# First mixer of a two-layer trunk: convolution input in a PSUM bank, one pair of convolution blocks inside the first pass, roots by eight heads, later transposes

## Chip, cores and metric

The kernel runs on one core of one Trainium2 chip. The metric is the device time of one execution in microseconds. Inputs and weights lie in device memory, in layouts that the kernel's packing on the host has chosen; that packing is not timed.

## What is computed

A trunk of two layers over 256 tokens of width 2048. Each layer is a mixer and a feed-forward network, each with an RMS norm whose scale, shift and gate come from a conditioning vector (`mod = silu(c) @ ada_w + ada_b`). The change lies in the first layer's mixer:

```python
def even_mixer(h, ...):
    z = h @ w_in
    a, q, kc, vc, ks, vs, kw, vw, gl = split_cols(z, EVEN_SPLITS)   # 2048, 1024, 6 x 256, 24
    y_a = conformer_conv(a, conv_w, conv_b, conv_ln_g, conv_ln_b)
    y_b = nsa_attention(q, kc, vc, ks, vs, kw, vw, gl, ...)
    return concatenate([y_a, y_b], axis=-1) @ w_out

def conformer_conv(a, w_dw, b_dw, ln_g, ln_b):
    a1, a2 = split(a, 2, axis=-1)                                   # value and gate, 1024 channels each
    y = causal_dwconv(a1 * sigmoid(a2), w_dw, b_dw)                 # 31 taps per channel, along the tokens
    return silu(layer_norm(y, ln_g, ln_b))
```

`nsa_attention` norms and rotates 8 heads of q and the keys k_sel and k_win (2 heads of 128 each), compresses k_cmp and v_cmp by a small network over windows of 32 tokens, and adds three gated attentions per head. All is float32.

## The kernel before

Tokens are one tile of 256 (NT = 2 halves of 128); channels go in blocks of 128 partitions, and the width of 2048 is 16 k-tiles. Activations `h(kt)` are kept transposed. `mm_t` (L350) makes a transposed output block, 128 channels by 256 tokens; `mm_n` (L361) makes outputs with tokens on the partitions.

**Weights.** `Weights` holds a list of loads in the order of use. `load_to` (L116) issues each from SyncE's queue into one of three `raw` buffers; `take` hands over the next piece and keeps the loads ahead. Conditioning weights come through the same queue: `ada()` (L263) reduces one 128x2048 tile on VectorE (L269), 192 times in all, and then issues the next load into the buffer just read (L260), so such a load waits on the queue for VectorE, with all that stands behind it.

**What sets the order.** Each engine runs its instructions in the order in which the program issues them. The helper `take` (L319) issues side work at each weight piece: deferred steps (`advance`), the next entry of the lists `hooks` and `beside` (`hook`), and by rate constants some `jobs` and some `ada()` (`tick`, L300). A rate of 0.5 is one per two takes. The constants at L55 to L80 are such rates, by stage.

**The first mixer, in order.**
1. The first pass (L776 to L787): one loop over the 16 k-tiles accumulates in eight PSUM banks: `oc` (two blocks of k_cmp, a bank each), `ok` (k_sel and k_win) and `oq` (q).
2. Four fills of convolution blocks. `fill` (L888) projects one block; the first of a pair is the gate (`sg`, tanh on ScalarE, L894), the second the value, after which `taps` (L899) writes `xp` = (sg + 1) * value (L904).
3. The values of the attention: `proj_n` with 268 columns, twice; beside it the keys and queries are finished: `squares` (ScalarE, L592), `roots` (L1021, one reciprocal root over all 24 heads on VectorE), `scaled` (L596), `roped` (two products on GpSimd, then L605 and L606 on VectorE), `turned_in` (transposes on PE, L613). All these stand in `hooks`, one per take; the three `turned_in` are entries 9, 11 and 13.
4. Two blocks of v_cmp, the compression of k_cmp (`hidden`, L849; `hs`, L861), two fills, that of v_cmp.
5. Ten fills, and beside them the heads: `stage_a` and `stage_b`, one per take. They hold the scores, the exponentials (L1173) and the transposes, whose results are copied by VectorE (`pT`, L1198) and ScalarE (L1199, L1200), then PE's outputs (L1209).
6. The output projection, whose first blocks need attention only; then the sums for the layer norm of the convolution (`cs`, L979; PE's L986), and the rest.

**A convolution block** takes 31 taps of 128x256, each reading a shifted window of `xp`, cut into six jobs: 10 taps by ScalarE (`pr`, L919), which GpSimd adds up (`yp`, L921), and 21 by VectorE into two accumulators in turn (`cy`, `ye`; L926, L928, L930). `xp` lies in SBUF in two buffers, so `taps` forces only the jobs of the block before last:

```python
            while c > 1 and c - 2 not in tapped:
                jobs.pop(0)()
            xp = xps[c % 2]
```

Of the kernel before, what the change touches and what calls it, by code (L numbers as in the profile page):

```python
# [54 lines left out]
LO_A = 0.25  # L55
ADA_A = 0.25
CONV_A = 0
CONV_1 = 0.7
CONV_2 = 2.0
CONV_3 = 1.2  # L60
CONV_OUT = 4
PRE = 5
SP = (7, 10)
# [2 lines left out]
LO_2 = 0.25  # L66
LO_3 = 0.25
LO_T = 0.25
ADA_T = 0.4
LO_F = 0.25  # L70
ADA_1 = 0.5
ADA_2 = 0.5
ADA_3 = 0.6
ADA_F0S = 0.45
ADA_F0U = 0.42
ADA_F0D = 0.22
ADA_L1 = 0.0
# [75 lines left out]
def trunk(ctx, tc, a, out):  # L153
# [6 lines left out]
    wp = ctx.enter_context(tc.tile_pool(name="wp", bufs=3))  # L160
    hm = ctx.enter_context(tc.tile_pool(name="hm", bufs=12))
    sm = ctx.enter_context(tc.tile_pool(name="sm", bufs=2))
    psum = ctx.enter_context(tc.tile_pool(name="psum", bufs=8, space=bass.MemoryType.PSUM))

    def bank():
        return psum.tile([P, 512], F32, tag="bank", name="bank")


    cc = const.tile([P, 3, P], F32, name="cc")
# [35 lines left out]
                W.want(a["wdn"][i, q, kt], QK, P)  # L205

    for kt in range(KD):
        W.want(a["ev_1"][kt], 1, 1792, cuts=(768, 1024), split=False)
    def want_pairs(c0, c1):
        for c in range(c0, c1):  # L210
            for ab in (1, 0):
                W.want(a["ev_a"][2 * c + ab], KD, P, split=False)
# [2 lines left out]
        for u in range(4):  # L215
            W.want_raw(a["cmp_w1"][kv, :, u * 2048:(u + 1) * 2048], 2048)

    want_pairs(0, 2)
    for c in range(2):
        W.want(a["ev_v"][c], KD, 268, split=False)  # L220
    for g in range(2):
# [121 lines left out]
    def mm_t(o, w, s_, x, start, stop):  # L343
        if isinstance(w, tuple):
            hi, lo = w
            PE.matmul(o, hi[:, s_], x[:, 0], start=start, stop=False)  # L346
            PE.matmul(o, hi[:, s_], x[:, 1], start=False, stop=False)  # L347
            PE.matmul(o, lo[:, s_], x[:, 0], start=False, stop=stop)  # L348
        else:
            PE.matmul(o, w[:, s_], x, start=start, stop=stop)  # L350

    def mm_n(o, w, s_, x, start, stop):
        for t in range(NT):
            ts_ = slice(t * P, (t + 1) * P)
            if isinstance(w, tuple):
                hi, lo = w
                PE.matmul(o[t], x[:, 0, ts_], hi[:, s_], start=start, stop=False)
                PE.matmul(o[t], x[:, 0, ts_], lo[:, s_], start=False, stop=False)
                PE.matmul(o[t], x[:, 1, ts_], hi[:, s_], start=False, stop=stop)
            else:  # L360
                PE.matmul(o[t], x[:, ts_], w[:, s_], start=start, stop=stop)  # L361
# [232 lines left out]
    def head_scale(z, nh, r, gain, n):  # L594
        for h in range(nh):
            V.scalar_tensor_tensor(n[:, h], z[:, h], r[:, h:h + 1], gain(h), op0=ALU.mult, op1=ALU.mult)  # L596
# [134 lines left out]
    nc.sync.dma_start(posi, a["pos"])  # L731
    nc.sync.dma_start(inv, a["inv"].partition_broadcast(P))
    V.memset(onesm, 1.0)
    make_identity(nc, ident)

    for u in range(4):
# [33 lines left out]
    table = tables()  # L770
    h = Modulated(0, 0, whole=True)
    h.bc = on_all(token_rstd())
    oc = [bank()[:, :T] for _ in range(2)]
    ok = [bank() for _ in range(NT)]
    oq = [[bank() for _ in range(NT)] for _ in range(2)]
    for kt in range(KD):  # L776
        x = h(kt)
        if kt > 1:
            next(table, None)
        first, stop = kt == 0, kt == KD - 1  # L780
        w, _ = take()
        for g in range(2):
            mm_t(oc[g], w, slice(g * P, (g + 1) * P), x, first, stop)
        mm_n(ok, w, slice(256, 768), x, first, stop)
        w, _ = take()
        for c in range(2):
            mm_n(oq[c], w, slice(c * 512, (c + 1) * 512), x, first, stop)  # L787
# [9 lines left out]
    with tc.tile_pool(name="l0", bufs=2) as lp:  # L797
# [81 lines left out]

        ys = []  # L880
        glu = []
        xps = [lp.tile([P, 30 + T], F32, name=f"xp{u}", bufs=1) for u in range(2)]
        for xp in xps:
            G.memset(xp[:, :30], 0.0)
        norm = {}
        count, totals, tapped = [0], [], set()

        def fill():  # L888

            o = proj_t(h)  # L890
            if count[0] % 2 == 0:
                sg = lp.tile([P, T], F32, tag="sg", name="sg")
                glu.append(sg)
                defer(lambda: S.activation(sg, o, AF.Tanh, scale=0.5))  # L894
            else:
                defer(lambda: taps(o))
            count[0] += 1

        def taps(o):  # L899
            c = len(ys)  # L900
            while c > 1 and c - 2 not in tapped:
                jobs.pop(0)()
            xp = xps[c % 2]
            V.scalar_tensor_tensor(xp[:, 30:], glu.pop(0), 1.0, o, op0=ALU.add, op1=ALU.mult)  # L904

            y = lp.tile([P, T], F32, tag="cy", name="cy", bufs=8)
# [101 lines left out]
        def activated(c):  # L1008
            S.activation(mix(c), ys[c], AF.Silu, bias=cvw[:, c, 33:34], scale=cvw[:, c, 32:33])
# [7 lines left out]
        def squares(i):  # L1017
            for u in (2 * i, 2 * i + 1):
                head_squares(zs[u], 4, s24[:, u])

        def roots():  # L1021
            flat = s24.rearrange("p a b -> p (a b)")
            V.tensor_scalar(flat, flat, 1.0 / P, EPS, op0=ALU.mult, op1=ALU.add)
            r = rsqrt(flat, 24)
            V.tensor_scalar(r[:, 8:], r[:, 8:], SCALE, None, op0=ALU.mult)
            root.append(r)

        def scaled(i):
            n = hm.tile([P, NT, 4, P], F32, tag="hm", name="n")
            ns.append(n)  # L1030
            gain = (lambda j: gains[:, 0]) if i else (lambda j: gains[:, 2 + j // 2])
            for t in range(NT):
                u = 2 * i + t
                head_scale(zs[u], 4, root[0][:, 4 * u:4 * u + 4], gain, n[:, t])

        later = []

        def roped_rest():
            while later:
                later.pop(0)()  # L1040
# [13 lines left out]
                    S.activation(qT[i - 1][:, :, t * P:(t + 1) * P], p, AF.Copy)  # L1054

        hooks.append(lambda: (squares(0), adds[0]()))
        hooks.append(lambda: (squares(1), adds[1]()))
        hooks.append(lambda: (squares(2), masks()))
        hooks.append(roots)
        hooks.append(lambda: scaled(0))  # L1060
        hooks.append(lambda: (scaled(1), roped(0)))
        hooks.append(lambda: (scaled(2), roped_rest()))
        hooks.append(lambda: roped(1))
        hooks.append(lambda: (turned_in(0), roped_rest()))
        hooks.append(lambda: roped(2))
        hooks.append(lambda: (turned_in(1), roped_rest()))
        hooks.append(None)
        hooks.append(lambda: turned_in(2))
        rate.update(ada=ADA_A, jobs=CONV_A)
        W.share = LO_A  # L1070
        for _ in range(4):
            fill()
        rate.update(ada=ADA_1, jobs=CONV_1)
        W.share = LO_1
# [175 lines left out]
        def ready(c):  # L1250
# [3 lines left out]
            if c < 7:  # L1254
# [2 lines left out]
        drain()  # L1257
        rest = out_first(0, mix, 1, [finish, None, layer_stats, layer_scale, lambda: normed(0),
                                      lambda: (normed(1), activated(0))], ready, ADA_OUT)

    h = ffn(0, rest, None, ADA_F0S, ADA_F0U, ADA_F0D)

# [228 lines left out]
def layout(inputs):  # L1491
# [48 lines left out]
    w = x["ev_w_in"][0]  # L1540
    s = dict(zip("a q kc vc ks vs kw vw gl".split(), np.split(w, np.cumsum([2048, 1024] + [256] * 6), axis=1)))
    a["ev_a"] = blocks(s["a"]).reshape(2, 8, P, D).transpose(1, 0, 2, 3).reshape(16, P, D)
    a["ev_1"] = np.concatenate([s["kc"], s["ks"], s["kw"], s["q"]], axis=1).reshape(KD, P, 1792)
    v = np.concatenate([s["vs"], s["gl"], s["vw"]], axis=1)
    a["ev_v"] = np.stack([rows(v[:, :268]), rows(v[:, 268:])])
    a["ev_c"] = blocks(s["vc"])
# [42 lines left out]
```

## Time and profile before

| what | before |
|---|---|
| runs, median (lowest to highest of 3) | 2412.89 us (2411.61 to 2413.17) |
| the profiled execution | 2410.45 us, its span 2408.7 us |
| PE busy | 2303.3 us, 96% |
| VectorE, ScalarE, GpSimd busy | 1663.0, 1029.5, 575.0 us |
| moved by DMA | 597.66 MB |
| first mixer, first pass to the sums of the convolution | 30.8 to 430 us of the span |

Times of the trace count from the start of the span. In a timeline row stand the start, the length, the engine, the line, the operation with its tiles, and xN where N like instructions are one row; a float32 matmul is two records, so a block of 16 products is 32 records. In square brackets stands how long the engine had been idle and what released it.

### The profile page before, as it was taken

What the parts mean: (1) busy time and instruction counts of PE and PEld (TensorE: products, weight loads), DVE (VectorE), ACT (ScalarE), POOL (GpSimd) and SP (SyncE); (2) the same over time, 40 slices, a digit from 0 to 9 for tenths busy, and PEclk for the clock granted to TensorE, in tenths of its full rate; (3) what the DMA queues carried; (4) which work ended last, traced back from release to release, by engine and by line L of the source; (5) the groups of instructions that cost most, each with busy time, mean ns of one, the idle gap of its engine ahead of it and who ended that gap; (6) DMA issues with size and microseconds to landing.
All of it is one profiled execution on the core that took longest, in us unless ns stands there. A gap on an engine that the chain in (4) does not pass through costs nothing. (4 is left out here: it accounts for less than half of the span.)

```text
span 2408.7 us, 39982 instructions
## 1 busy us (share of the span) xinstructions
PE 2303.3 (96%) x16052; PEld 2134.6 (89%) x16052; DVE 1663.0 (69%) x2587; ACT 1029.5 (43%) x1803; POOL 575.0 (24%) x329
## 2 busy tenths in 40 slices
PE   6899999898999999999999999999999999999999
PEld 3476778788999999999999877999999999999999
DVE  7758689738968877877887467555786554554554
ACT  2021253125434544544544545446534444444443
POOL 4233534001322222222222131110222212222221
PEclk9999999999999999999999999999999999999999
DMA  9968754866879878878888542444577545545545
GB/s 387 427 224 334 300 187 166 307 226 261 334 273 355 329 275 334 341 274 315 345 309 295 194 158 105 156 168 179 214 269 271 191 156 201 186 157 204 182 165 169
DMA packets 96525, 597.66 MB, mean 248 GB/s; under 512 B 11345, under 2 KB 14033, under 8 KB 44241
## 3 DMA queue, kind: packets, MB, share of 16 engines
q1 hardware_dynamic: 96338, 595.10, 66.8%
q8 instruction: 126, 2.06, 0.3%
q14 instruction: 61, 0.50, 0.1%
HBM read 592.96 MB, written 2.10 MB: 247 GB/s over the span
## 5 line engine op out<-in xcount | busy, mean ns | idle before, releaser
L133 ACT ACTIVATE whi<-raw 128x1024 fp32r<-128x1024 f32 (+2 forms) x659 | 626.4, 952 | 859.1 <-PE bank L347 727.9
L139 DVE TENSOR_TENSOR wlo<-raw,whi 128x1024 fp32r<-128x1024 f32 (+2 forms) x495 | 560.1, 1133 | 410.5 <-ACT whi L133 410.2
L139 POOL TENSOR_TENSOR wlo<-raw,whi 128x1024 fp32r<-128x1024 f32 (+2 forms) x164 | 389.4, 2374 | 1558.8 <-ACT whi L133 1504.5
L348 PE MATMUL bank<-h,wlo 128*128 128x256 f32 x2624 | 745.7, 284 | 9.5 <-DVE wlo L139 8.7
L346 PE MATMUL bank<-h,whi 128*128 128x256 f32 x2624 | 745.4, 284 | 0.0
L347 PE MATMUL bank<-h,whi 128*128 128x256 f32 x2624 | 744.7, 284 | 0.0
L348 PEld LDWEIGHTS bank<-h,wlo 128*128 128x128 f32 x2624 | 506.0, 193 | 10.8 <-DVE wlo L139 9.8
L346 PEld LDWEIGHTS bank<-h,whi 128*128 128x128 f32 x2624 | 506.3, 193 | 0.1
L347 PEld LDWEIGHTS bank<-h,whi 128*128 128x128 f32 x2624 | 506.2, 193 | 0.1
L269 DVE CUSTOM_DVE_ANT_0 ada<-ada,cB,adab 128x2048 f32<-128x2048 f32 x192 | 462.5, 2412 | 28.9 <-DMA ada<-adaw 28.2
L347 PE MATMUL bank<-g,whi 128*128 128x256 f32 x1408 | 403.4, 286 | 8.7 <-DVE g L662 8.5
L346 PE MATMUL bank<-g,whi 128*128 128x256 f32 x1408 | 402.9, 286 | 6.7 <-ACT g L661 5.9
L348 PE MATMUL bank<-g,wlo 128*128 128x256 f32 x1408 | 403.5, 287 | 4.4 <-DVE wlo L139 3.1
L347 PEld LDWEIGHTS bank<-g,whi 128*128 128x128 f32 x1408 | 274.3, 195 | 10.3 <-DVE g L662 10.3
L346 PEld LDWEIGHTS bank<-g,whi 128*128 128x128 f32 x1408 | 274.2, 195 | 7.7 <-ACT g L661 6.7
L348 PEld LDWEIGHTS bank<-g,wlo 128*128 128x128 f32 x1408 | 274.4, 195 | 6.4 <-DVE wlo L139 3.8
L350 PE MATMUL bank<-hw,raw 128*128 128x256 f32 x640 | 149.0, 387 | 10.7 <-DMA raw<-ev 7.9
L350 PEld LDWEIGHTS bank<-hw,raw 128*128 128x128 f32 x640 | 121.5, 194 | 38.9 <-issue 18.3
L350 PE MATMUL bank<-hr,raw 128*128 128x257 f32 x640 | 140.4, 380 | 0.0
L650 DVE SCALAR_TENSOR_TENSOR y<-bank,fcw,y 128x255 f32<-128x255 f32 x162 | 77.4, 478 | 90.2 <-ACT y L649 90.2
L350 PEld LDWEIGHTS bank<-hr,raw 128*128 128x128 f32 x640 | 121.0, 190 | 16.6
L350 PE MATMUL bank<-mixw,raw 128*128 128x256 f32 x512 | 115.7, 389 | 6.5 <-DMA raw<-out 6.5
(261 smaller groups left out, 2492.5 us busy)
## 6 DMA issues: line engine op xcount, KB each, us to landing
ada<-adaw SPq DMA_DIRECT2D x192, 1024.0 KB, 5.8
raw<-wup SPq DMA_DIRECT2D x162, 1024.0 KB, 6.3
raw<-wdn SPq DMA_DIRECT2D x128, 704.0 KB, 4.8
raw<-out SPq DMA_DIRECT2D x44, 512.0 KB, 4.2
raw<-ev_a SPq DMA_DIRECT2D x16, 1024.0 KB, 5.6
raw<-ev SPq DMA_DIRECT2D x16, 896.0 KB, 14.7
raw<-wup SPq DMA_DIRECT2D x16, 896.0 KB, 4.5
raw<-cmp_w SPq DMA_DIRECT2D x8, 1024.0 KB, 9.2
```

Source lines behind the costliest of these rows:

```text
L133: nc.scalar.activation(hi[:, :n], raw, AF.Copy)
L139: eng.tensor_sub(lo[:, :n], raw, hi[:, :n].bitcast(F32))
L269: V.tensor_tensor_reduce(w, w, cB, 1.0, adab[:, i * 96 + j:i * 96 + j + 1], ALU.mult, ALU.add, m)
L346: PE.matmul(o, hi[:, s_], x[:, 0], start=start, stop=False)
L347: PE.matmul(o, hi[:, s_], x[:, 1], start=False, stop=False)
L348: PE.matmul(o, lo[:, s_], x[:, 0], start=False, stop=stop)
L350: PE.matmul(o, w[:, s_], x, start=start, stop=stop)
L650: V.scalar_tensor_tensor(y[:, 1:], o[:, :T - 1], w[:, 1:2], y[:, 1:], op0=ALU.mult, op1=ALU.add)
```

## The change

- `xp` lies in PSUM, one bank of its own (pool `xq`), in place of two buffers in SBUF. Until the end of the first mixer the other pool has seven banks. With one `xp`, `taps` forces all jobs of the block before. Its 30 leading columns are zeroed by VectorE, not GpSimd.
- The first pass takes convolution pair 0 (gate and value block) along: 2048 columns a k-tile for 1792, four `mm_t` for two. Two blocks share a bank, which a product of zeros opens. The first two fills take these results; two fills follow in place of four, and two loads of `ev_a` go.
- In the first pass the load of the next weights is issued ahead of the next `h(kt)`, and so ahead of the ada loads that this issues.
- `roots(i)` per eight heads, three times for once; `turned_in(i)` moves to the list `beside`, entries 10 to 12.
- Rates: ada 0.35 for 0.5 (beside the values), 0.7 for 0.6 (beside the heads), 0.5 for 0.4 and 0.5 for 0.45 (behind them); conv jobs 0.8 for 0.7 and 1.75 for 1.2.

```diff
-CONV_1 = 0.7
+CONV_1 = 0.8
-CONV_3 = 1.2
+CONV_3 = 1.75
-ADA_T = 0.4
+ADA_T = 0.5
-ADA_1 = 0.5
+ADA_1 = 0.35
-ADA_3 = 0.6
+ADA_3 = 0.7
-ADA_OUT = 0.45
+ADA_OUT = 0.5
...
-        W.want(a["ev_1"][kt], 1, 1792, cuts=(768, 1024), split=False)
+        W.want(a["ev_1"][kt], 1, 2048, cuts=(1024, 1024), split=False)
-    want_pairs(0, 2)
+    want_pairs(1, 2)
...
-    oc = [bank()[:, :T] for _ in range(2)]
+    oc = [xq.tile([P, 512], F32, tag="xp", name="oc"), bank()]
+    for o in oc:
+        PE.matmul(o, zero[:, :P], zero, start=True, stop=False)
+    oc = [o[:, u * T:(u + 1) * T] for o in oc for u in range(2)]
...
     for kt in range(KD):
+        W.load_to(kt + 2)
         x = h(kt)
...
-        for g in range(2):
-            mm_t(oc[g], w, slice(g * P, (g + 1) * P), x, first, stop)
-        mm_n(ok, w, slice(256, 768), x, first, stop)
+        for g in range(4):
+            mm_t(oc[g], w, slice(g * P, (g + 1) * P), x, False, stop and g % 2 == 1)
+        mm_n(ok, w, slice(512, 1024), x, first, stop)
...
-        def fill():
-            o = proj_t(h)
+        def fill(o=None):
+            if o is None:
+                o = proj_t(h)
...
-            while c > 1 and c - 2 not in tapped:
+            while c and c - 1 not in tapped:
                 jobs.pop(0)()
-            xp = xps[c % 2]
+            if not xps:
+                xps.append(xq.tile([P, 512], F32, tag="xp", name="xp")[:, :30 + T])
+                V.memset(xps[0][:, :30], 0.0)
+            xp = xps[0]
...
-        hooks.append(lambda: (squares(1), adds[1]()))
-        hooks.append(lambda: (squares(2), masks()))
-        hooks.append(roots)
-        hooks.append(lambda: scaled(0))
-        hooks.append(lambda: (scaled(1), roped(0)))
-        hooks.append(lambda: (scaled(2), roped_rest()))
-        hooks.append(lambda: roped(1))
-        hooks.append(lambda: (turned_in(0), roped_rest()))
-        hooks.append(lambda: roped(2))
-        hooks.append(lambda: (turned_in(1), roped_rest()))
-        hooks.append(None)
-        hooks.append(lambda: turned_in(2))
+        hooks.append(lambda: (squares(1), roots(0), adds[1]()))
+        hooks.append(lambda: (squares(2), scaled(0), masks()))
+        hooks.append(lambda: (roots(1), scaled(1)))
+        hooks.append(lambda: (roots(2), scaled(2), roped(0)))
+        hooks.append(lambda: (roped_rest(), roped(1)))
+        hooks.append(lambda: (roped_rest(), roped(2)))
+        hooks.append(roped_rest)
+        beside.extend([None] * 9)
+        for i in range(3):
+            beside.append(lambda i=i: turned_in(i))
...
-        for _ in range(4):
+        fill(oc[2])
+        fill(oc[3])
+        advance()
+        for _ in range(2):
             fill()
```

**PE from the end of the first pass to the compression.** L350, after the change L359, is a block's product (16 a block); L361, later L370, the 268-column products of the values; L613, later L622, the transposes of `turned_in`. Before:

```order
L361 MATMUL bank<-raw,hw 128x512 x6
L350 MATMUL bank<-hw,raw 128x256 x64
L613 MATMUL bank<-ident,n 128x128 x8
L361 MATMUL bank<-raw,hw 128x268 x8
L613 MATMUL bank<-ident,n 128x128 x8
L361 MATMUL bank<-raw,hw 128x268 x10
L613 MATMUL bank<-ident,n 128x128 x8
L361 MATMUL bank<-raw,hw 128x268 x46
L350 MATMUL bank<-hw,raw 128x256 x32
```

With the change:

```order
L359 MATMUL oc<-hw,raw 128x256 x2
L359 MATMUL bank<-hw,raw 128x256 x2
L370 MATMUL bank<-raw,hw 128x512 x6
L359 MATMUL bank<-hw,raw 128x256 x32
L370 MATMUL bank<-raw,hw 128x268 x22
L622 MATMUL bank<-ident,n 128x128 x8
L370 MATMUL bank<-raw,hw 128x268 x6
L622 MATMUL bank<-ident,n 128x128 x8
L370 MATMUL bank<-raw,hw 128x268 x4
L622 MATMUL bank<-ident,n 128x128 x8
L370 MATMUL bank<-raw,hw 128x268 x32
```

Two blocks lie between the pass and the values for four, and the first transposes come after 22 products of the values, which before followed them.

**VectorE at the first convolution block.** L904 and L922 write `xp`; L605 and L606 are the rotation; L926 to L930, later L944 to L948, are taps. Before, the rotations stand between the write and the taps, and four taps are done before the third:

```order
L904 SCALAR_TENSOR_TENSOR xp_581<-sg,bank 128x256 [waits PE_49,Activation_49]
L605 TENSOR_TENSOR n<-n,cc 128x512 [waits Pool_49]
L606 TENSOR_TENSOR n<-n,nrw 128x512 [waits DVE_49]
L605 TENSOR_TENSOR n<-n,cc 128x512 [waits Pool_49]
L606 TENSOR_TENSOR n<-n,nrw 128x512 [waits DVE_49]
L926 TENSOR_SCALAR cy<-xp_580,cvw 128x256 [waits DMAHW6_49]
L928 TENSOR_SCALAR ye<-xp_580,cvw 128x256
L930 SCALAR_TENSOR_TENSOR cy<-xp_580,cvw,cy 128x256 [waits DVE_49]
L930 SCALAR_TENSOR_TENSOR ye<-xp_580,cvw,ye 128x256 [waits DVE_49]
```

With the change the 21 taps of block 0 stand in one run (its first twelve rows with the ada reduction ahead), and behind the run the next `xp`, the third root and only then the rotations:

```order
L278 ISA ada,mod<-ada,cB,adab 128x2048 [waits DMAHW0_49]
L278 ISA mod 128x1
L944 TENSOR_SCALAR cy<-xp,cvw 128x256 [waits DMAHW6_49,Activation_49,Pool_49]
L946 TENSOR_SCALAR ye<-xp,cvw 128x256
L948 SCALAR_TENSOR_TENSOR cy<-xp,cvw,cy 128x256 [waits DVE_49]
L948 SCALAR_TENSOR_TENSOR ye<-xp,cvw,ye 128x256 [waits DVE_49]
L948 SCALAR_TENSOR_TENSOR cy<-xp,cvw,cy 128x256 [waits DVE_49,Activation_49]
L948 SCALAR_TENSOR_TENSOR ye<-xp,cvw,ye 128x256 [waits DVE_49]
L948 SCALAR_TENSOR_TENSOR cy<-xp,cvw,cy 128x256 [waits DVE_49]
L948 SCALAR_TENSOR_TENSOR ye<-xp,cvw,ye 128x256 [waits DVE_49]
L948 SCALAR_TENSOR_TENSOR cy<-xp,cvw,cy 128x256 [waits Activation_49]
L948 SCALAR_TENSOR_TENSOR ye<-xp,cvw,ye 128x256 [waits DVE_49]
```

The rotations, which PE's first transposes wait for, have moved behind the run; and a tap in it waits for ScalarE at the start of each job, which none does before.

**ScalarE in attention.** L919, later L937, are its taps; L1199 and L1200, later L1219 and L1220, the copies of a head's transposed weights. Before:

```order
L919 ACTIVATE yp<-xp_580,cvw 128x256 [waits DVE_49]
L919 ACTIVATE pr<-xp_580,cvw 128x256 [waits Pool_49]
L1211 ACTIVATE mixw<-bank 128x256 [waits PE_49]
L1199 ACTIVATE pT<-bank 128x256 [waits PE_49]
L1200 ACTIVATE pC<-bank 15x256 [waits PE_49]
L1159 ACTIVATE sc<-bank 128x256
L919 ACTIVATE pr<-xp_580,cvw 128x256 [waits Pool_49] x2
```

With the change:

```order
L937 ACTIVATE yp<-xp,cvw 128x256 [waits DVE_49]
L937 ACTIVATE pr<-xp,cvw 128x256 [waits Pool_49]
L937 ACTIVATE pr<-xp,cvw 128x256 [waits DVE_49,Pool_49]
L937 ACTIVATE pr<-xp,cvw 128x256 [waits Pool_49]
L937 ACTIVATE pr<-xp,cvw 128x256 [waits DVE_49,Pool_49]
L1231 ACTIVATE mixw<-bank 128x256 [waits PE_49]
L1219 ACTIVATE pT<-bank 128x256 [waits PE_49]
L1220 ACTIVATE pC<-bank 15x256 [waits PE_49]
L1179 ACTIVATE sc<-bank 128x256
L937 ACTIVATE pr<-xp,cvw 128x256 [waits DVE_49,Pool_49]
```

The first tap of each job now waits for VectorE's taps of the job before, and the copies stand behind it on the queue.

## Rows read from the trace of the kernel before

**Rows 1.** waits of PE by source, 140 to 620 us: total, times, longest

```profile
PE bank L350 <- DMA raw<-out: 6.5, 3, 3.3
PE bank L986 <- DVE cs L979: 5.9, 1, 5.9
PE bank L361 <- DMA raw<-ev_v: 3.3, 1, 3.3
PE bank L866 <- DVE hs L861: 3.1, 1, 3.1
PE bank L1209 <- DVE pT L1198: 3.0, 1, 3.0
PE bank L613 <- DVE n L606: 2.8, 2, 2.2
PE bank L849 <- DMA raw<-cmp_w: 2.1, 2, 1.8
```

**Rows 2.** busy time in a stretch: its length, PE, PEld, DVE, ACT, POOL, clock, DMA, GB/s

```profile
400.00:420.00 20.00, 16.69 (x78) 14.41 (x77) 19.93 (x35) 4.98 (x12) 9.17 (x12) 1.00 0.39 150
```

**Rows 3.** timeline of PE, first pass and after: start, length, instructions, [idle before <-releaser]

```profile
30.77 2.08 PE L350 MATMUL bank<-hw,raw 128*128 128x256 f32 x4 [2.57 <-ACT hw L511]
...
45.06 1.03 PE L350 MATMUL bank<-hw,raw 128*128 128x256 f32 x4
45.92 5.31 PE L361 MATMUL bank<-raw,hw 128*128 128x512 f32 x12
51.07 1.03 PE L350 MATMUL bank<-hw,raw 128*128 128x256 f32 x4
...
121.37 1.10 PE L350 MATMUL bank<-hw,raw 128*128 128x256 f32 x4 [0.80 <-DMA raw<-ev]
...
139.48 27.79 PE L350 MATMUL bank<-hw,raw 128*128 128x256 f32 x128
...
181.11 19.14 PE L361 MATMUL bank<-raw,hw 128*128 128x268 f32 x84
```

**Rows 4.** the page, the span in 40 slices of 60.2 us: what DMA moved

```profile
GB/s 387 427 224 334 300 187 166 307 226 261 334 273 355 329 275 334 341 274 315 345 309 295 194 158 105 156 168 179 214 269 271 191 156 201 186 157 204 182 165 169
```

**Rows 5.** timeline of VectorE behind the first pass

```profile
140.35 2.24 DVE L836 TENSOR_TENSOR ab<-cmpz,pe 128x240 f32<-128x240 f32 x4 [18.51 <-DMA pe<-cmp_pos]
...
150.28 0.18 DVE L397 TENSOR_SCALAR rsi<-s 128x24 int32<-128x24 int32 x1
150.49 0.18 DVE L398 TENSOR_SCALAR rsy<-rsi 128x24 int32<-128x24 int32 x1
...
155.34 6.29 DVE L596 SCALAR_TENSOR_TENSOR n<-bank,rsy,gains 128x128 f32<-128x128 f32 x24
161.55 0.68 DVE L605 TENSOR_TENSOR n<-n,cc 128x512 f32<-128x512 f32 x1
...
187.33 0.47 DVE L930 SCALAR_TENSOR_TENSOR cy<-xp,cvw,cy 128x256 f32<-128x256 f32 x1
187.72 0.47 DVE L930 SCALAR_TENSOR_TENSOR ye<-xp,cvw,ye 128x256 f32<-128x256 f32 x1
```

**Rows 6.** VectorE by line and form, 139 to 430 us: busy us, mean ns, idle before

```profile
L269 DVE CUSTOM_DVE_ANT_0 ada<-ada,cB,adab 128x2048 f32<-128x2048 f32 x33 | 81.0, 2458 | 7.7 <-DMA ada<-adaw 7.7
L930 DVE SCALAR_TENSOR_TENSOR cy<-xp,cvw,cy 128x256 f32<-128x256 f32 x80 | 49.4, 618 | 0.0
```

**Rows 7.** line 650 over the whole span: duration in ns, min/median/max

```profile
L650 DVE SCALAR_TENSOR_TENSOR y<-bank,fcw,y x162: 468/478/486, 587.9 to 2342.1; 128x255 f32<-128x255 f32 x162
```

**Rows 8.** timeline of ScalarE in attention, taps of one conv block

```profile
289.55 0.51 ACT L919 ACTIVATE yp<-xp,cvw 128x256 f32<-128x256 f32 x1 [0.20 <-DVE xp L904]
289.97 1.69 ACT L919 ACTIVATE pr<-xp,cvw 128x256 f32<-128x256 f32 x4
```

**Rows 9.** timeline of PE behind attention

```profile
430.18 5.83 PE L350 MATMUL bank<-mixw,raw 128*128 128x256 f32 x16
```

**Rows 10.** timeline of SyncE's queue behind attention

```profile
405.82 0.33 SPq L260 DMA_DIRECT2D ada<-adaw  x1
```

More of the change, by code (lines that the diff above doesn't have):

```diff
@@ L162, in trunk, with all_banks @@
     sm = ctx.enter_context(tc.tile_pool(name="sm", bufs=2))
-    psum = ctx.enter_context(tc.tile_pool(name="psum", bufs=8, space=bass.MemoryType.PSUM))
+    banks = [tc.tile_pool(name="xq", bufs=1, space=bass.MemoryType.PSUM),
+             tc.tile_pool(name="psum0", bufs=7, space=bass.MemoryType.PSUM)]
+    xq, psum = [p.__enter__() for p in banks]
     def bank():
         return psum.tile([P, 512], F32, tag="bank", name="bank")
+    def all_banks():
+        nonlocal psum
+        for p in reversed(banks):
+            p.__exit__(None, None, None)
+        psum = ctx.enter_context(tc.tile_pool(name="psum", bufs=8, space=bass.MemoryType.PSUM))
     cc = const.tile([P, 3, P], F32, name="cc")
@@ L733, in trunk @@
     V.memset(onesm, 1.0)
+    zero = hm.tile([P, 512], F32, tag="hm", name="zero")
+    V.memset(zero, 0.0)
     make_identity(nc, ident)
@@ L881, in trunk @@
         glu = []
-        xps = [lp.tile([P, 30 + T], F32, name=f"xp{u}", bufs=1) for u in range(2)]
-        for xp in xps:
-            G.memset(xp[:, :30], 0.0)
+        xps = []
         norm = {}
         count, totals, tapped = [0], [], set()
-        def fill():
-            o = proj_t(h)
+        def fill(o=None):
+            if o is None:
+                o = proj_t(h)
             if count[0] % 2 == 0:
@@ L1019, in squares, with roots @@
                 head_squares(zs[u], 4, s24[:, u])
-        def roots():
-            flat = s24.rearrange("p a b -> p (a b)")
+        def roots(i):
+            flat = s24[:, 2 * i:2 * i + 2].rearrange("p a b -> p (a b)")
             V.tensor_scalar(flat, flat, 1.0 / P, EPS, op0=ALU.mult, op1=ALU.add)
-            r = rsqrt(flat, 24)
-            V.tensor_scalar(r[:, 8:], r[:, 8:], SCALE, None, op0=ALU.mult)
+            r = rsqrt(flat, 8)
+            if i:
+                V.tensor_scalar(r, r, SCALE, None, op0=ALU.mult)
             root.append(r)
@@ L1033, in scaled @@
                 u = 2 * i + t
-                head_scale(zs[u], 4, root[0][:, 4 * u:4 * u + 4], gain, n[:, t])
+                head_scale(zs[u], 4, root[i][:, 4 * t:4 * t + 4], gain, n[:, t])
         later = []
@@ L1259, in trunk @@
                                       lambda: (normed(1), activated(0))], ready, ADA_OUT)
+    drain()
+    all_banks()
     h = ffn(0, rest, None, ADA_F0S, ADA_F0U, ADA_F0D)
@@ L1542, in layout @@
     a["ev_a"] = blocks(s["a"]).reshape(2, 8, P, D).transpose(1, 0, 2, 3).reshape(16, P, D)
[L1543 removed]
+    a["ev_1"] = np.concatenate([s["kc"], s["a"][:, 1024:1152], s["a"][:, :128], s["ks"], s["kw"], s["q"]], axis=1).reshape(KD, P, 2048)
     v = np.concatenate([s["vs"], s["gl"], s["vw"]], axis=1)
```

## Prediction

> **What bounds the kernel now.** I read the page's first part, then PE's waits by source in the first mixer, then the timelines of PE and VectorE around the places that the change touches. PE is busy for 96% of the span (the table above), so a gain is either matmul work that goes or one of PE's waits. The change touches only the first mixer (and some rates of the jobs that run beside it), and there the reader should see seven waits, 26.7 us together [rows 1]: three on loads (out, ev_v, cmp_w: 6.5, 3.3, 2.1) and four on VectorE (cs 5.9, hs 3.1, pT 3.0, n 2.8). VectorE explains those four: in 400 to 420 us it is busy for 19.93 of 20 us [rows 2]. So the first mixer is a stage in which PE and VectorE are both nearly full, and what one gains the other can take back.
>
> **Part 1, the first pass, +2.4.** A k-tile costs PE 6.02 us where nothing is waited for, the distance from the row at 45.06 to that at 51.07; its two 256-column products are the 4 records at 45.06, and 0.86 later the next product starts [rows 3]. Two more such products per k-tile are 16 x 0.86 = 13.8 us. But in the middle transfers set the pace: the k-tile at 121.37 began after 0.80 us without data [rows 3], the last of ten such waits, 7.9 us together. That much of the added work fills time that was idle. PE alone would need 16 x (6.02 + 0.86) = 110 us from 30.77, which with the opening's 1 us is 141.9 against 139.48: +2.4. The bounds: +1.5 if the first k-tiles' waits also vanish; +7 if transfers stay the bound, since 2 MB more (16 loads of 128 x 256 numbers) at the pace of the middle, 427 GB/s [rows 4], are 4.9 us and the last three k-tiles, which ran on data already there, add 3 x 0.86 on top. I take +2.4, since the order of the loads puts the ev load ahead of a pair of ada loads instead of behind it. The two zero matmuls stand in the 2.57 us that PE waits before 30.77; were they not hidden, they would cost 4 records at 5.15/12 = 0.43, 1.7 us [rows 3].
>
> **Part 2, two blocks less to fill, -13.9.** The row at 139.48 is four blocks in 27.79 us [rows 3]: half of it goes, with its two loads.
>
> **Part 3, the values wait for VectorE, +12.5.** PE now comes to the first turned_in after two blocks (13.9) and 22 products of 268 columns, 44 records at 19.14/84 = 0.228 us [rows 3], that is 10.0, and a bank that frees 0.7 late: 24.6 us after the pass. VectorE by its new order needs, from the same moment: the window adds of both groups, 2 x 1.1, half of the 2.24 each [rows 5]; roots of heads 0 to 7 and 8 to 15, 11 and 12 small operations at a pitch of 0.21, 2.4 and 2.6 [rows 5] (eight columns instead of 24 I take at the same price; the pitch is hardly the columns'); two scalings of eight, 8 x 0.262 = 2.1 each [rows 5]; one ada reduction at least 2.3, at 2.46 in the mean [rows 6]: 13.7 in all. Then the order puts the whole of conv block 0 in one run: 21 taps and the sum of the two accumulators, 22 at the pitch of 0.40 that free taps have [rows 5], 8.8, and its handshakes (Part 5), 4.7: 13.5. Then xp 0.4, the third root 2.6 and scaling 2.1, and the first rotation, four products and sums of 0.68 [rows 5], 2.7. That is 35.0, so PE waits 10.4 us where it waited for nothing; the next two turns cost 0.5 and 3.7 by the same count, the bank 0.7: 15.3, against 2.8 now [rows 1]. Bounds: nothing beyond today's 2.8 if the run hides behind PE's 24.6 us, +17 if each job of the run costs a microsecond more. The cause is that `taps` may not write the single xp before the block ahead has been tapped, so it forces six jobs ahead of the rotations.
>
> **Part 4, waits that go early, -5.7.** Two loads fewer ahead of them let ev_v land before it is wanted: -3.3 (the whole wait; its bounds 0 and -6, the clock behind it included). cmp_w gains from the lower rate of ada work, 2.1 to about 0.9, and hs, which waits for VectorE behind such work, 3.1 to 1.9: -1.2 each [rows 1].
>
> **Part 5, the taps.** xp now lies in PSUM. A tap costs 618 ns in the mean of 80, and its 73 twins on the other accumulator are alike [rows 6]; the same operation with its first operand in PSUM took 468 to 486 ns in all 162 instances [rows 7]. At 475 a tap, 153 x 0.144 = 22 us of VectorE, spread over all eight blocks. I read the gap as the taps that run beside GpSimd's adds of yp. Against this stands that ScalarE's taps and VectorE's no longer run together. Today ScalarE begins 0.20 us after xp is written and runs its taps at a pitch of 0.42 [rows 8] while VectorE taps the same tile. In the changed order the first VectorE tap of a job waits for ScalarE, and the first ScalarE tap of the next job for VectorE. With nothing between two jobs VectorE idles 0.20 + 2 x 0.42 = 1.04 us per job of two ScalarE taps, 0.62 for one: an estimate from these two rows. Lower bound 0, where other VectorE work lies between. Upper bound 2.2, where ScalarE has as much other work queued ahead as the five instructions of rows 8 take, 0.51 + 1.69.
>
> The Trainium skill ("PSUM — Partial Sum Buffer", section "PSUM bank collisions raise a hardware error") speaks against moving xp here: it says that ScalarE and VectorE must not touch the same bank in one cycle, reads included, so that the two sets of taps have to be ordered. No run before shows it, since both read xp from SBUF; by the rule the handshakes stay, without it their 4.7 and 6.0 us would go and the sum be -16.1.
>
> **Part 6, attention, +6.3.** From the first pT copy to the last VectorE now does 50 taps for 42 and 9 ada reductions for 7, by the counts of the order. 8 x 0.40 + 2 x 2.3 = +7.8; contention spared on 42 taps, -6.0; a dozen jobs of which half find nothing between, +6.0. So +7.8 on an engine that is full [rows 2]. Of the 3.0 us that PE waits for the first pT [rows 1] I take half as gone, because three ada reductions fewer stand ahead of it: -1.5.
>
> **Part 7, behind attention, -7.0.** The second half of the backlog shrinks: 35 taps instead of 44 between the last pT and cs, each cheaper. 44 x 0.62 = 27 us become 14 and 7 of handshakes, so cs is ready 6 us earlier: PE's wait of 5.9 goes, and with it the slow restart: the 16 products at 430.18 took 5.83 us [rows 9], where 16 of the row at 139.48 take 3.47 [rows 3]: -2.3. Against it: an ada load that waits for its buffer holds SyncE's queue, and the out loads behind it, at 405.82 [rows 10], and PE waits 3.3 for raw<-out [rows 1]; five now stand in front of such a load, one behind two of them: the 3.3 that this cost becomes 4.5, +1.2.
>
> **Sum.** 2.4 - 13.9 + 12.5 - 5.7 + 6.3 - 7.0 = -5.4 us against the profiled execution, 2410.45 us: 2405.0. The median of the runs shown is 2412.9, 2.4 above it, so **2407.5**. What the rates move between later stages I take as nothing: the 192 ada reductions stay the same, under the FFN's matmuls.
>
> **The rivals.**
> - *The handshakes lock both engines* (slower). In attention ScalarE's own copies of pT and pC stand behind a tap that waits for VectorE, and VectorE's taps behind ScalarE's exponentials. For it: the queues by their order. Against it: ScalarE is not busy. At 2.2 us in each of a dozen jobs they cost 26 us for 6; of these 20 some 12 reach PE, since it has only the waits of Part 7 to give: 2419.5. It decides from about 1.0 us in every job, double my sum, where 5.4 us more eat the forecast's gain.
> - *VectorE keeps up.* The jobs find other work between them, a handshake costs 0.3. Then Part 3 is 6 less, Part 6 about 5 less: -16.5, **2396.4**. For it: 22 us of VectorE are freed. Against: the run of block 0 has nothing between its jobs.
> - *The first pass stays bound by its transfers*, +7 for +2.4: -0.8, 2412, no change. For it: ten waits for data in the middle of the pass; against it: the ev load is now queued earlier.
>
> **How the numbers follow.** A measurement of this kernel can tell about 0.2% (4.8 us) from no change. The forecast has 0.40, the lock 0.22, VectorE keeping up 0.16, the transfers 0.22. The forecast's own spread, some 6 us, lies half beyond 0.2%: faster 0.24 + 0.16 + 0.05 = 0.45; slower 0.20 + 0.07 = 0.27; the rest 0.28. The range reaches from VectorE keeping up to a little beyond the lock: 2395 to 2421; the likeliest case alone 2401 to 2414.
>
> **What would show it.** Right: the pass ends near 142 us; a wait of PE for n at the first turn near 10 us, with 21 taps in a row on VectorE ahead of it; taps at 477 ns; the cs wait gone. Wrong: waits of VectorE for ScalarE's pr of over 1 us in every job (the lock), or waits for raw<-ev on to the end of the pass (the transfers), or no wait at the first turn (VectorE keeps up).

## The result and the profile after

The change makes the kernel slower: 2425.31 us in the median of 4 runs (2424.59 to 2427.66) against 2413.03 us (2411.61 to 2414.98), a ratio of 1.0063, with a 95% interval of 1.0048 to 1.0078. The forecast was 2407.5 us in a range of 2395 to 2421: the measured time lies beyond it, on the side of the first rival. The profiled execution with the change took 2427.66 us, its span is 2425.9.

The waits of PE with the change, 140 to 620 us (the first mixer and the start of the feed-forward network behind it), answer to [rows 1] (total, times, longest):

```profile
PE bank L622 <- DVE n L615: 18.4, 5, 12.3
...
PE bank L1214 <- ACT mixw L1231: 6.6, 3, 2.8
PE bank L359 <- DMA raw<-out: 4.3, 2, 2.6
PE bank L1229 <- DVE pT L1218: 3.4, 2, 2.2
...
PE bank L359 <- ACT mixw L1231: 2.3, 1, 2.3
PE bank L882 <- DVE hs L877: 1.4, 1, 1.4
...
PE bank L865 <- DMA raw<-cmp_w: 0.6, 1, 0.6
```

The waits that the prediction removed are gone or smaller: cs and ev_v have no row left, hs fell from 3.1 to 1.4, cmp_w from 2.1 to 0.6. Two are larger: n grew from 2.8 to 18.4, and 8.9 us (6.6 and 2.3) stand at ScalarE's copies of `mixw`, which had no row. The timeline of PE with the change, at the joints of the stages:

```profile
143.38 7.07 PE L359 MATMUL bank<-hw,raw 128*128 128x256 f32 x32
...
157.93 10.10 PE L370 MATMUL bank<-raw,hw 128*128 128x268 f32 x44
180.35 1.08 PE L622 MATMUL bank<-ident,n 128*128 128x128 f32 x4 [12.32 <-DVE n L615]
...
196.64 15.56 PE L370 MATMUL bank<-raw,hw 128*128 128x268 f32 x64
212.03 13.98 PE L359 MATMUL bank<-hw,raw 128*128 128x256 f32 x64
...
310.65 1.63 PE L1229 MATMUL bank<-pT,vn 128*128 128x128 f32 x8 [2.17 <-DVE pT L1218]
...
398.53 3.45 PE L359 MATMUL bank<-mixw,raw 128*128 128x256 f32 x12
404.32 25.30 PE L359 MATMUL bank<-mixw,raw 128*128 128x256 f32 x116 [2.34 <-ACT mixw L1231]
...
524.00 9.26 PE L359 MATMUL bank<-hr,raw 128*128 128x257 f32 x42
```

The same joints of the kernel before, as far as they are not in [rows 3]:

```profile
167.11 1.04 PE L613 MATMUL bank<-ident,n 128*128 128x128 f32 x8
...
207.24 14.97 PE L350 MATMUL bank<-hw,raw 128*128 128x256 f32 x64
...
311.24 1.75 PE L1209 MATMUL bank<-pT,vn 128*128 128x128 f32 x8 [2.98 <-DVE pT L1198]
...
384.37 24.34 PE L350 MATMUL bank<-mixw,raw 128*128 128x256 f32 x112
...
515.05 9.26 PE L350 MATMUL bank<-hr,raw 128*128 128x257 f32 x42
```

The row with `hr` is the first product of the feed-forward network, so 515.05 and 524.00 end the first mixer: +9.0 us there. Each stage is a difference of two joints ("first pT" is the first product that waits for VectorE's copy):

| stage | joints before, after | forecast | measured |
|---|---|---|---|
| first pass | to 139.48, to 143.38 | +2.4 | +3.9 |
| fills up to the values | 27.6, 14.55 | -13.9 | -13.1 |
| values, without the wait for ev_v (3.3) | 36.9, 54.1 | +12.5 | +17.2 |
| the wait for ev_v | 3.3, 0 | -3.3 | -3.3 |
| to the first pT | 104.0, 98.6 | -3.9 | -5.4 |
| attention, to the first output product | 73.1, 87.9 | +7.8 | +14.8 |
| output projection | 130.7, 125.5 | -7.0 | -5.2 |
| sum | | -5.4 | +8.9 |

The first five rows together are -0.6 (310.65 against 311.24). PE has as many products as before, since the two blocks only moved into the first pass, where they fill time in which it had waited for data; so it came to the values 9.2 us earlier (157.93 for 167.11), and nearly all of that was back as waits before the first head. What makes the kernel slower in the mixer is attention. VectorE's waits with the change, 140 to 440 us, say what attention waits for:

```profile
DVE cy L948 <- ACT pr L937: 21.4, 27, 1.0
...
DVE cy L944 <- ACT pr L937: 10.1, 5, 5.2
```

Before, no wait of VectorE for `pr` has a row. And the taps themselves (VectorE by line and form, 139 to 440 us), as [rows 6]:

```profile
L948 DVE SCALAR_TENSOR_TENSOR cy<-xp,cvw,cy 128x256 f32<-128x256 f32 x80 | 38.2, 478 | 21.4 <-ACT pr L937 21.4
L948 DVE SCALAR_TENSOR_TENSOR ye<-xp,cvw,ye 128x256 f32<-128x256 f32 x73 | 34.6, 474 | 0.0
```

A tap is as fast as forecast, 478 and 474 ns for 618 and 624. That is 22 us saved, and 31.5 us of waits in their place.

### The profile page after: what moved, and what is told of

It reads as the page before. It is cut to its first block, busy times and chain, and to the rows that moved or that the text cites. A ratio compares the mean times of both kernels' runs of the same rounds, so it can differ in the third digit from the quotient of the medians.

```text
span 2425.9 us, 40074 instructions
## 1 busy us (share of the span) xinstructions
PE 2308.9 (95%) x16056; PEld 2135.9 (88%) x16056; DVE 1647.5 (68%) x2614; ACT 1027.0 (42%) x1803; POOL 552.0 (23%) x327
## 4 chain that ended last, share of the span: by engine, by line
PE 74%; DVE 14%; DMA 5%; ACT 3%; issue 2%; POOL 1%; SPq 0%; ACTq 0%; DVEq 0%
PE bank L357 19%; PE bank L356 19%; PE bank L355 19%; PE bank L359 9%; PE bank L370 3%; DVE ada L278 3%; DMA ada<-adaw 2%; DVE wlo L139 2%; DVE cy L948 1%; POOL wlo L139 1%; DVE ye L948 1%; PE bank L366 1%; PE bank L368 1%; PE bank L367 1%; ACT whi L133 1%
## 5 line engine op out<-in xcount | busy, mean ns | idle before, releaser
L139 DVE TENSOR_TENSOR wlo<-raw,whi 128x1024 fp32r<-128x1024 f32 (+2 forms) x495 | 567.7, 1148 | 412.9 <-ACT whi L133 412.7
L139 POOL TENSOR_TENSOR wlo<-raw,whi 128x1024 fp32r<-128x1024 f32 (+2 forms) x164 | 399.6, 2437 | 1566.5 <-ACT whi L133 1506.4
L355 PEld LDWEIGHTS bank<-g,whi 128*128 128x128 f32 x1408 | 274.1, 195 | 14.2 <-ACT g L670 13.1
L359 PE MATMUL bank<-hr,raw 128*128 128x257 f32 x640 | 140.4, 380 | 0.0
L359 PE MATMUL bank<-hw,raw 128*128 128x256 f32 x576 | 135.7, 389 | 0.5 <-ACT sg L909 0.5
L359 PEld LDWEIGHTS bank<-hr,raw 128*128 128x128 f32 x640 | 121.0, 190 | 16.6
L359 PEld LDWEIGHTS bank<-hw,raw 128*128 128x128 f32 x576 | 110.9, 195 | 17.9 <-issue 1.7
L359 PE MATMUL bank<-mixw,raw 128*128 128x256 f32 x512 | 114.6, 386 | 9.2 <-DMA raw<-out 4.3
```

Source lines behind the costliest of these rows:

```text
L139: eng.tensor_sub(lo[:, :n], raw, hi[:, :n].bitcast(F32))
```

## The experiments

One number beside the runs' ratios is used throughout, the end of the first mixer (the first product with `hr`) in each profiled execution: what comes behind it differs between these kernels by some microseconds in either direction for reasons of its own (below). It comes from one execution of each kernel and has no interval. Ratios are to the kernel before, on the same chip. No ratio is further than 1.4% from 1; what is called faster or slower below has an interval that leaves out 1.

| kernel | ratio (95% interval) | median us, before beside it | end of first mixer, us (before 515.05) |
|---|---|---|---|
| the change | 1.0063 (1.0048 to 1.0078) | 2425.3, 2413.0 | 524.0, +9.0 |
| two SBUF buffers | 1.0041 (1.0024 to 1.0059) | 2419.2, 2408.5 | 516.3, +1.3 |
| one SBUF buffer | 1.0111 (1.0091 to 1.0131) | 2436.7, 2408.5 | 531.2, +16.2 |
| old rates | 1.0074 (1.0051 to 1.0097) | 2427.3, 2408.5 | 525.0, +10.0 |
| twin | 0.9959 (0.9943 to 0.9975) | 2400.1, 2408.5 | 495.7, -19.4 |
| two SBUF buffers, old rates | 1.0003 (0.9992 to 1.0015) | 2411.1, 2409.2 | 508.6, -6.4 |
| pair alone | 1.0007 (0.9996 to 1.0018) | 2409.5, 2409.2 | 511.9, -3.1 |
| twin, late fills | 0.9934 (0.9912 to 0.9955) | 2393.1, 2409.2 | 490.5, -24.6 |
| twin, old rates | 0.9976 (0.9962 to 0.9990) | 2404.8, 2409.2 | 504.4, -10.6 |
| the change, late fills | 1.0014 (1.0001 to 1.0028) | 2414.3, 2411.1 | 511.7, -3.4 |
| one ScalarE tap | 1.0055 (1.0041 to 1.0070) | 2424.6, 2411.1 | 520.5, +5.4 |
| twin, one fill ahead | 0.9866 (0.9841 to 0.9892) | 2378.9, 2411.1 | 485.2, -29.9 |
| before with the twin | 0.9972 (0.9957 to 0.9988) | 2404.4, 2411.1 | 512.7, -2.4 |

**Two SBUF buffers for xp.**

```diff
-            while c and c - 1 not in tapped:
+            while c > 1 and c - 2 not in tapped:
...
-            if not xps:
-                xps.append(xq.tile([P, 512], F32, tag="xp", name="xp")[:, :30 + T])
-                V.memset(xps[0][:, :30], 0.0)
-            xp = xps[0]
+            xp = xps[c % 2]
```

> The changed kernel with xp back in two SBUF buffers (and so only the block before last forced), everything else of the change kept. Theory A: the loss comes from the single xp in a PSUM bank, by the turns that ScalarE and VectorE take on it (31.5 us of VectorE's waits in the changed kernel) and by the run of block 0 that is forced ahead of the rotations. Then the first pass keeps its gain of about 10 us, the 12.3 us wait at the first transposes falls below 3, VectorE's waits for pr go, and the time is about 2400 us, under the kernel before. Theory B: the loss lies in the roots by eight, the later transposes or the pair in the first pass; then the time stays above 2417. Theory C: the rates; above 2417 too.

A miss: 2419 us where 2400 was expected. VectorE's waits for `pr` are gone as expected, the first transposes no longer wait, and the first mixer is 7.7 us shorter than with the change; but it is no better than before: PE still waits 9.0 us for n, now at the later transposes (longest 6.0), and 7.4 for pT. That part of theory A falls which held that everything but the bank is a gain.

**One SBUF buffer.** As above, but `c - 1` and one buffer.

> The changed kernel with xp in one SBUF buffer: the block before is still forced, but both engines may read at once and GpSimd's adds contend again. Theory A says how the loss divides: what this gains on the changed kernel is the price of the turns in PSUM less the contention saved, what the two-buffer kernel gains on this one is the price of forcing. I expect about 2412 us: the wait at the first transposes near 12 us stays, the waits of the transposes for the copies of mixw (6.6 us) go. Theory B and C: 2422 or more.

A miss by 25 us: the slowest kernel of all. So PSUM as such is no loss. With the same forcing, the bank with its turns is 7.2 us better in the mixer than one SBUF buffer; and forcing, one buffer against two, costs 14.9 us there. VectorE has no waits for `pr` here, and its taps are slower (by line and form):

```profile
L947 DVE SCALAR_TENSOR_TENSOR cy<-xp,cvw,cy 128x256 f32<-128x256 f32 x80 | 54.9, 686 | 0.0
L947 DVE SCALAR_TENSOR_TENSOR ye<-xp,cvw,ye 128x256 f32<-128x256 f32 x73 | 49.2, 674 | 0.0
```

That is 104.1 us for 72.8 with the change: 31.3 us more, as much as the 31.5 us of waits that went. The slow taps are those beside GpSimd, as Part 5 read it. In the trace of the kernel before, the 75 taps with no GpSimd instruction beside them took 470 to 480 ns, the other 78 took 760 in the mean; here 93 have one beside them, and took 813.

**Old rates.** The six constants of the kernel before.

> The changed kernel with all six rates of the kernel before. Theory C: the rates cause the loss, and the time falls to 2417 us or less. Theory A: they only move work between stages that VectorE fills anyway, 2425 us within 4; in attention fewer waits (fewer taps beside the heads), behind it more (cs late).

As theory A said: +10.0 for +9.0. Theory C falls for the kernel as changed. In 300 to 400 us VectorE's waits for `pr` fall from 13.6 to 7.6 us, and behind attention PE waits 9.7 us for one copy of `mixw`.

**The twin.**

```diff
-            V.scalar_tensor_tensor(xp[:, 30:], glu.pop(0), 1.0, o, op0=ALU.add, op1=ALU.mult)
+            xa, sg = xas[c % 2], glu.pop(0)
+            V.scalar_tensor_tensor(xa[:, 30:], sg, 1.0, o, op0=ALU.add, op1=ALU.mult)
+            V.scalar_tensor_tensor(xp[:, 30:], sg, 1.0, o, op0=ALU.add, op1=ALU.mult)
...
-                    S.activation(pr, xp[:, j:j + T], AF.Copy, scale=cvw[:, c, j:j + 1])
+                    S.activation(pr, xa[:, j:j + T], AF.Copy, scale=cvw[:, c, j:j + 1])
```

> The changed kernel with xp written twice by VectorE, once into the PSUM bank, from which VectorE alone taps, and once into one of two SBUF buffers, from which ScalarE alone taps. No engine waits for the other over a bank, a tap of VectorE stays at 476 ns, the forced run stays, 8 writes of 0.42 us come on top. Theory A: the turns are the larger part of the loss; VectorE's waits for pr vanish, the wait at the first transposes falls from 12.3 to about 8 us, and the time is about 2410 us. If moving xp to PSUM were a loss apart from the turns (the forcing alone), the time stays above 2418 us.

This is the experiment that decides. Of the change only the turns are taken away, 3.4 us of extra writes come on top, and the mixer is 28.3 us shorter, the time 1.0% lower, 10 us better than expected. VectorE's waits for `pr` have no row, and the taps stay fast (by line and form):

```profile
L953 DVE SCALAR_TENSOR_TENSOR cy<-xp,cvw,cy 128x256 f32<-128x256 f32 x80 | 38.0, 475 | 0.0
```

PE's waits for n fall from 18.4 to 9.8 us, those for `mixw` from 8.9 to 2.3 (waits of PE, twin kernel):

```profile
PE bank L622 <- DVE n L615: 9.8, 4, 5.0
...
PE bank L1219 <- ACT mixw L1236: 2.3, 3, 1.2
```

**Two SBUF buffers with the old rates.** The first kernel with the six constants of before.

> The changed kernel with xp in two SBUF buffers and all six rates of the kernel before; left of the change are the pair in the first pass, the roots by eight and the later transposes. The two-buffer kernel with the new rates was 10.7 us slower than before, and its PE waits for VectorE in attention (pT 7.4 us). Theory D: the new rates ask more of VectorE beside the heads than it can do while its taps contend with GpSimd; with the old rates the time falls by 8 us or more, to 2404 to 2411 us. Theory B (roots and later transposes, or the pair itself, cost the time): it stays at 2415 us or more.

Theory D holds: 7.7 us of the mixer were the new rates, which ask for more taps beside the heads than a VectorE with contending taps can do. What is left of the change, the pair, the roots, the later transposes and seven banks for eight, comes to 1.0003.

**The pair alone,** in the kernel before: the columns in the first pass, two fills fewer, nothing else.

> The kernel before with the pair in the first pass alone (two fills fewer ahead of the values, load order of the change in the pass), roots, transposes and rates as before. The pass gives 10 us on PE. Theory D: VectorE is the bound up to the sums of the convolution, so most comes back as waits (at the first transposes, at the first pT): 2403 to 2410 us. If PE's work were the bound: 2400 us or less. Theory B with the pair itself as the cost: 2413 us or more.

1.0007: nothing in the time, although PE is through with the pass and the fills 10.9 us earlier (156.22 for 167.11). At the end of the mixer 3.1 are left. The waits of PE for this kernel show where they went, against 2.8 for n and 5.9 for cs in [rows 1]:

```profile
PE bank L613 <- DVE n L606: 12.5, 5, 5.8
PE bank L350 <- ACT hr L475: 6.1, 1, 6.1
...
PE bank L993 <- DVE cs L986: 5.8, 1, 5.8
```

9.7 more at n; and 6.1 at the start of the feed-forward network, where the next modulation is not ready. The ada reductions go by takes, and two fills fewer are fewer takes: at the end of the first mixer 75 reductions are done here and in the three other kernels with the pair and the old rates, which wait 5 to 6 us at that place too. All other kernels have 76 or 77 done, and none waits there.

**The twin with late fills.** The second pair's fills, with their loads, behind the values, the transposes four takes later.

```diff
-        beside.extend([None] * 9)
+        beside.extend([None] * 13)
...
-        for _ in range(2):
-            fill()
         rate.update(ada=ADA_1, jobs=CONV_1)
...
             defer(lambda o=o, c=c: values(o, c))
+        for _ in range(2):
+            fill()
```

> The twin kernel (ScalarE's taps from SBUF) with the fills of the second pair behind the products of the values and the transposes four takes later, so that no block of taps is forced ahead of the rotations. If the forced run is what still costs (waits of 9.8 us for n in the twin kernel), they fall below 3 us and the time is about 2393 us. If the run only moves, VectorE's taps come back as waits in attention, and the time stays at 2398 us or more.

2393.1 us, as expected: no transposes wait for n any more. One wait is new, 6.8 us at the first product of the values, whose bank VectorE has yet to free.

**The twin with the old rates.**

> The twin kernel with all six rates of the kernel before. Theory D says that the new rates suit taps that do not contend: with the old ones fewer taps lie beside the heads and the sums of the convolution come late; 2403 us or more. If the rates are of no matter: 2400 us within 3.

Theory D again: here the new rates are worth 8.7 us of the mixer, where the two-buffer kernel lost 7.7 by them.

**The change with late fills.** The same edit on the changed kernel.

> The changed kernel, xp in the one PSUM bank for both engines, with only the placing of the late twin kernel: the second pair's fills behind the values, the transposes four takes later. It tells the price of the turns by itself. The forced run ahead of the rotations goes, and with it most of the 18.4 us of waits for n; the turns stay in attention. If the turns cost mainly through the forced run, the time is near the late twin kernel, 2397 us or less. If they cost in attention as well (VectorE's waits for pr, and ScalarE's copies of mixw behind a waiting tap), about half of the 25 us between the changed kernel and the twin is left: 2405 to 2413 us.

2414.3 us, 1 above the second range: the mixer is 12.3 us shorter than with the change, and still 21.2 longer than the twin in the same order. With the forced run that distance was 28.3, so the turns cost more outside the run than in it. PE's waits for n nearly go (18.4 to 0.3, with 6.6 new at the bank as in the late twin), and those for `mixw` grow from 8.9 to 13.3. Busy time in attention, 300 to 400 us, this kernel and then its twin (length, PE, PEld, DVE, ACT, POOL, clock, DMA, GB/s):

```profile
300.00:400.00 100.00, 83.92 (x420) 68.78 (x420) 81.60 (x204) 50.30 (x173) 33.70 (x42) 0.95 0.45 159
```

```profile
300.00:400.00 100.00, 96.16 (x486) 81.03 (x487) 90.45 (x216) 50.37 (x167) 42.84 (x49) 0.98 0.56 205
```

With the turns, PE, VectorE and GpSimd all do less in the same time, and ScalarE no more: no engine is full, they wait for each other.

**One tap on ScalarE.** `TAPS_ACT` 1 for 10, `TAPS_LAST` 1 for 9, the job rates by 4/3.

> The changed kernel with one tap of a block on ScalarE in place of ten (nine in the last), thirty on VectorE, GpSimd's adds gone, and the rates of the jobs raised by 4/3 since a block has eight jobs for six. VectorE gains 9 taps a block (72 x 0.40 = 28 us) and loses some 27 us of its waits for pr: the same load. If the loss of the change is VectorE's time alone: 2425 us within 4. If ScalarE's queue is what locks PE (copies of mixw and pT behind a tap that waits), those waits of 9 us go with the turns: 2417 us or less.

2424.6 us, the number of the first reading, but the load was not equal: VectorE's taps take 106.1 us for 72.8, and 8.1 of its waits for ScalarE stay of 31.5, so it carries 10 us more than with the change and the mixer is yet 3.5 us shorter. The waits for `mixw` fall to 1.8 us and those for pT grow from 3.4 to 8.9. The copies behind waiting taps are then one form in which PE meets a late VectorE, and no separate cause that this run could show.

**The twin with one fill ahead.** Of the two late fills the gate block goes ahead of the values again, into the 6.8 us wait; the transposes come two takes later still (15 empty entries for 13).

> The late twin kernel with one of the two late fills, the gate block, moved ahead of the values again. In the late twin kernel PE waits 6.8 us for a bank at the first product of the values, since VectorE has not yet scaled the first heads; this block has a bank and fills that time. 2387 to 2391 us if the wait only cost PE; 2393 us within 2 if it comes back as a wait for n or in attention.

2378.9 us, 1.3% under the kernel before, the best of all and 8 us below the lowest time expected. No wait for n or for that bank is left. 5.3 us of the 14 between this and the late twin lie in the first mixer, the rest in later stages, which was not expected and is not explained.

**The kernel before with the twin alone.**

> The kernel before with the twin xp alone: VectorE taps from one PSUM bank, ScalarE from two SBUF buffers, the block before forced; first pass, roots, transposes and rates as before. By the freed 22 us of VectorE less the forcing, 2401 to 2406 us. If the gain of the twin kernels comes from the pair in the first pass instead, 2409 us within 4.

2404.4 us, in the range expected, 0.28% faster: fast taps are worth something without the pair. (The profiled execution, of 2410.6 us, is one of the longer ones.) The pair without fast taps is worth nothing, and the two together, with the new rates, the roots by eight and a fitting order, 1.3%.

## Why the prediction was wrong

**Part 5 and 6, the price of the turns, failed.** The prediction had the mechanism: VectorE's first tap of a job waits for ScalarE, 0.62 to 1.04 us a job. It put 4.7 us in the forced run (five turns at its own two prices are 4.4); 4.0 were measured, in five waits. The fourth job's:

```profile
164.80 0.47 DVE L948 SCALAR_TENSOR_TENSOR ye<-xp,cvw,ye 128x256 f32<-128x256 f32 x1
166.24 0.48 DVE L948 SCALAR_TENSOR_TENSOR cy<-xp,cvw,cy 128x256 f32<-128x256 f32 x1 [0.96 <-ACT pr L937]
```

For attention the sum had "a dozen jobs of which half find nothing between, +6.0". In that stage VectorE waited 12.0 us for `pr` (waits of VectorE, 309.9 to 398.5 us):

```profile
DVE cy L944 <- ACT pr L937: 7.9, 3, 5.2
DVE cy L948 <- ACT pr L937: 4.1, 5, 1.0
```

The five are of the forecast size. The three stand at the first tap of a block, where ScalarE has a head's work queued ahead. The prediction kept that case for the rival, with an upper bound of 2.2; the longest took 5.2:

```profile
385.33 0.54 DVE L944 TENSOR_SCALAR cy<-xp,cvw 128x256 f32<-128x256 f32 x1 [5.21 <-ACT pr L937]
```

So the turns took 6.0 us more than the sum had, and the stage was missed by 7.0, about half of the 14.3 us by which the whole mixer was missed. The sum also left out the turns between the forced run and attention, 8.0 us in ten waits. Those behind attention it had: 7 in Part 7, 7.6 measured. Over the mixer that is 31.5 us in 32 waits for 17.7 forecast. One turn in the three queues of attention, VectorE first:

```profile
314.03 0.42 DVE L922 SCALAR_TENSOR_TENSOR xp<-sg,bank 128x256 f32<-128x256 f32 x1
316.22 0.54 DVE L944 TENSOR_SCALAR cy<-xp,cvw 128x256 f32<-128x256 f32 x1 [1.76 <-ACT pr L937]
...
318.90 0.48 DVE L948 SCALAR_TENSOR_TENSOR cy<-xp,cvw,cy 128x256 f32<-128x256 f32 x1 [0.97 <-ACT pr L937]
```

ScalarE:

```profile
313.99 1.48 ACT L1207 ACTIVATE sc<-sc,su 128x128 f32<-128x128 f32 x4
315.37 0.45 ACT L937 ACTIVATE yp<-xp,cvw 128x256 f32<-128x256 f32 x1
...
318.03 0.84 ACT L937 ACTIVATE pr<-xp,cvw 128x256 f32<-128x256 f32 x2 [1.85 <-DVE ye L948]
320.65 0.47 ACT L937 ACTIVATE pr<-xp,cvw 128x256 f32<-128x256 f32 x1 [1.79 <-DVE ye L948]
321.03 0.38 ACT L1231 ACTIVATE mixw<-bank 128x256 f32<-128x256 f32 x1
```

PE:

```profile
321.46 1.11 PE L1214 MATMUL bank<-ident,sc 128*128 128x128 f32 x4 [2.84 <-ACT mixw L1231]
```

`xp` is written at 314.45. ScalarE first ends a head's scaling, so VectorE starts to tap at 316.22. Each set of taps then lets the other one go, and the copy of `mixw`, which frees the bank that PE needs, stands behind the last.

**The rule weighed in Part 5.** The Trainium skill ("PSUM — Partial Sum Buffer", section "PSUM bank collisions raise a hardware error") has the two engines ordered on a bank. No run here let them read one bank together, so the rule itself is not shown; its price is. Without turns the prediction's sum was -16.1 us, and the twin ends the first mixer 19.4 us before the kernel before.

**The first rival was right in sign and in mechanism, not in size.** It named this lock and its place, and 1.0 us in every job as the point from which it decides. The mean of the 32 waits is 0.98, but 16 of the 48 jobs have none; in attention it is 12.0 us for 54 taps, some 13 jobs, 0.9 each, far from the 2.2 that it was priced at. That its 2419.5 us was only 6 short is in part luck: it put 12 us more into attention, where 7.0 came, and the rest came in the values and behind the mixer. The chance of 0.22 was too low, since the argument against it, that ScalarE is not busy, does not bear on it: its queue runs in order, and a wait in it needs no load.

**Part 3** had the place and the cause. Forecast 10.4 us at the first transposes, measured 12.3; 15.3 at all of them, measured 18.4. The products behind the gaps are slower too: 15.56 us for 64 is 0.243 each where 0.228 was taken, 1.0 us. The granted clock was 0.94 over these products and 0.80 from 157.93 to 180.35 us, which holds the wait of 12.3, so PE ran part of the time at the lower of its two levels (1.2 for 2.4 GHz). Around both, 140 to 210 us, it is 0.88, the last number but two (columns as above):

```profile
140.00:210.00 70.00, 51.09 (x216) 40.82 (x215) 58.00 (x133) 20.51 (x76) 31.89 (x40) 0.88 0.43 143
```

**Parts 1, 2 and 4** held within 1.5 us. Of the 1.5 in Part 1, 1.1 lie ahead of the pass: its first product starts at 31.91 for 30.77, behind a load (`normg`) that VectorE waited 1.99 us for, before 0.91; the zero products are hidden, as taken. The first pass ran at PE's pace, 6.88 us a k-tile, with two waits for data of 0.26 and 0.25: the rival of the transfers is out. **Part 7** gave 5.2 of its 7.0: the wait for cs is gone, but 2.3 us stand at a copy of `mixw` instead.

**The last sentence of the sum,** nothing between later stages, was also wrong. Behind the first mixer the changed kernel loses 8.2 us more in the two profiled executions (524.00 - 515.05 = 9.0 of 17.2), and by the medians about 3. The eleven other kernels with the pair stand between 1.6 better and 10.3 worse than at the mixer's end. For the old rates a cause is shown, the late modulation at the start of the feed-forward network; for the others it is open.

## What to carry to other kernels

Before a tile that two engines read moves into a bank, count the turns that they will take on it and bound each by the longest stretch of work that either queue can hold ahead, not by the engines' load. A second write of 0.42 us, so that each engine reads its own copy, gave 28 us here, its cost of 3.4 already paid. Time won on PE is worth little while another engine is late at the next joint (the pair alone: 10.9 us won up to the values, 3.1 left at the end of the mixer, 1.0007 in all); free that engine first, then set the rates of side work and the order anew, since the same rates cost 7.7 us with contending taps and gave 8.7 with free ones.

## What the runs showed of the hardware

With VectorE's first operand in PSUM, its taps no longer show the spread of the kernel before: 466 to 486 ns for 465 to 1014. The spread was the taps beside a GpSimd instruction, 760 ns in the mean for 476 without one; from PSUM it is 477 and 474. GpSimd gains as well: its adds of `yp` take 727 ns in the median and 2769 at most, for 789 and 10720 before. A tap of ScalarE is a little shorter from PSUM too, 469 ns for 498 in the mean. Of 153 taps GpSimd runs beside 78 in the kernel before, where the mean is 618 ns, and beside 93 with one SBUF buffer, where it is 686.
